# A transformer layer's last normalization: one column block of the last row tile, and one step of the other tile, over GpSimd and ScalarE

## The chip, the core and the metric

The kernel runs on one core of a Trainium2 chip. A core has a matrix engine (TensorE, PE in the profile, with its weight loads as PEld), a vector engine (VectorE, DVE), a scalar engine (ScalarE, ACT), a general engine (GpSimd, POOL) and SyncE (SP), which here only issues transfers. The engines run side by side, each through its own list of instructions in order, and wait for each other by semaphores. The metric is the device time of one execution in microseconds; lower is better.

## The reference

One encoder layer on 256 rows of width 2048: attention, a normalization, an MLP of width 8192, a second normalization. What matters here is the last line, the second normalization:

```python
def layer_norm(x, g, b):
    xf = x.astype(jnp.float32)
    mu = jnp.mean(xf, axis=-1, keepdims=True)
    var = jnp.mean(jnp.square(xf - mu), axis=-1, keepdims=True)
    y = (xf - mu) * lax.rsqrt(var + LN_EPS)
    return (y * g.astype(jnp.float32) + b.astype(jnp.float32)).astype(x.dtype)
...
        y = sq_relu_mlp(hff, mlp_w1[i], mlp_b1[i], mlp_w2[i], mlp_b2[i])
        x = layer_norm(DEEPNORM_ALPHA * x + (1.0 + g_f[:, None, :]) * y, ln_mlp_g[i], ln_mlp_b[i])
```

## The kernel before

The 256 rows are two row tiles of 128 rows (t = 0 and 1), one row on each partition. The 2048 columns are four column blocks of 512 (c = 0 to 3). `part(xs, t, c)` is one such piece, 128x512 in float32. `xs` has one buffer for each c, with both row tiles in it: in the listings of instructions g_2615 is c = 0, g_2617 is c = 1, g_2619 is c = 2 and g_2621 is c = 3. Most of the kernel is a stream of weights from HBM, split into a high and a low part by ScalarE and VectorE, with three matmuls of TensorE for each product (`mm3`, lines 556 to 558). This case is about its last 15 us.

There the last products of the MLP come out for c = 3, first for row tile 0, then for row tile 1. Those of row tile 1 are finished in two halves of 256 columns, so that the sums of the first half can be taken while TensorE works on the second. `add_gated` (lines 836 to 844) multiplies a product by the gate into `tmp` (line 841), adds it to the row (842) and takes its statistics (844). Then the row tile is closed:

- Row tile 0: `deviation` (lines 860 to 875) makes the mean and variance `mv` from the statistics (864), the root `sd` on ScalarE (866), and a refined reciprocal root `qq` by three small VectorE steps (871, 873, 874). Line 1358 makes (z - mean) * g for each block, line 1359 multiplies by `rstd` and adds b, and `store` (1342 to 1344) writes the block out. These are scalar_tensor_tensor instructions on VectorE: two tensors and one number for each row.
- Row tile 1: three blocks (c = 0, 1, 2) go over TensorE. `scaled` (1346) has put -z * g / 2 in place earlier, line 1384 copies it into PSUM by a product with the identity, and line 1397 adds mean * g / 2 by a product with `dm`, a diagonal matrix of the means (line 1391). Line 1398 then multiplies by `rstd` and adds b. The fourth block, c = 3, comes too late for this. For it line 1392 makes (z - mean) * `gneg` on VectorE while ScalarE takes the root, where `gneg` is -g / 2 (line 1364), and line 1398 multiplies and adds as for the others. The order of the blocks is 3, 1, 2, 0.

What sets the order: the framework's scheduler orders each engine's list by its own estimates of cost. `high_priority(200)` puts the statistics of row tile 1 ahead of older work, and `keep_in_program_order` (`keep`, `kept`) fixes the order of the closing steps on their engines. Nothing fixes the order of the stores. Odd c are issued from SP, even c from ScalarE (line 1343), and each queue issues them in the order of its list: a store that waits holds back those behind it. The program ends when the last store has landed.

Of the kernel before, what the change touches and what calls it, by code (L numbers as in the profile page):

```python
# [14 lines left out]
AF = mybir.ActivationFunctionType  # L15
OP = mybir.AluOpType
# [45 lines left out]
def hybrid_kernel(ctx: ExitStack, tc: tile.TileContext, a, out: bass.AP):  # L62
    nc = tc.nc
# [23 lines left out]
    def g4(dt=F32):  # L87
        return gen.tile([128, 1024], dt, tag="g4", name="g4")
# [102 lines left out]
    def first(name):  # L191
        n = AHEAD.get((stage[0], name), AHEAD.get(name))
        return tc.high_priority(n) if n else nullcontext()
# [356 lines left out]
    acc, xts, held, xs = {}, {}, {}, [None] * 4  # L550

    def part(tiles, t, c):
        return tiles[c][:, t * 512:t * 512 + 512]
# [303 lines left out]
    def kept(i):  # L857
        return tc.keep_in_program_order(i) if tight[0] else i

    def deviation(st=None, mv=None, between=lambda: None):  # L860
        with first("deviation"):
            if mv is None:
                mv = sml.tile([128, 2], F32, name="mv")
                kept(nc.vector.bn_aggr(mv, st))
            sd = sml.tile([128, 1], F32, name="sd")
            kept(nc.scalar.activation(sd, mv[:, 1:2], AF.Sqrt, bias=eps))
            ve = sml.tile([128, 1], F32, name="ve")
            kept(nc.vector.tensor_scalar_add(ve, mv[:, 1:2], LN_EPS))
            between()
            r0 = sml.tile([128, 1], F32, name="r0")  # L870
            kept(nc.vector.reciprocal(r0, sd))
            q = sml.tile([128, 1], F32, name="qq")
            kept(nc.vector.scalar_tensor_tensor(q, r0, ve, r0, op0=OP.mult, op1=OP.mult))
            kept(nc.vector.scalar_tensor_tensor(q, q, -3.0, r0, op0=OP.add, op1=OP.mult))
        return mv, q
# [463 lines left out]
    def affine(c):  # L1339
        return (gb[n][c // 2][:, (c % 2) * 512:(c % 2) * 512 + 512] for n in range(2))  # L1340

    def store(t, c, z):
        q = nc.sync if c % 2 else nc.scalar
        q.dma_start(out[t * 128:t * 128 + 128, c * 512:c * 512 + 512], z)
# [9 lines left out]
    mv, rstd = deviation(st[0][:, :4])  # L1354
    nc.vector.tensor_scalar_mul(rstd, rstd, -0.5)
    for c in (1, 0, 2, 3):
        z, (g, b) = part(xs, 0, c), affine(c)
        nc.vector.scalar_tensor_tensor(z, z, mv[:, 0:1], g, op0=OP.subtract, op1=OP.mult)
        nc.vector.scalar_tensor_tensor(z, z, rstd, b, op0=OP.mult, op1=OP.add)
        store(0, c, z)  # L1360
    for c in range(3):
        scaled(1, c)
    gneg = sml.tile([128, 512], F32, name="w", tag="t2", bufs=4)
# [17 lines left out]
    pw = {}  # L1381
# [4 lines left out]
    keep = tc.keep_in_program_order  # L1386
    with tc.high_priority(200):
        mv = sml.tile([128, 2], F32, name="mv")
        keep(nc.vector.bn_aggr(mv, st[1][:, :5]))
        dm = sml.tile([128, 128], F32, name="dm", tag="t2", bufs=4)  # L1390
        keep(nc.vector.tensor_scalar(dm, ident, mv[:, 0:1], 0.5, op0=OP.mult, op1=OP.mult))
        rstd = deviation(mv=mv, between=lambda: keep(nc.vector.scalar_tensor_tensor(
            part(xs, 1, 3), part(xs, 1, 3), mv[:, 0:1], gneg, op0=OP.subtract, op1=OP.mult)))[1]
    for c in (3, 1, 2, 0):
        z, (g, b) = part(xs, 1, c), affine(c)
        if c < 3:
            nc.tensor.matmul(pw[c], dm, g, start=False, stop=True)
        keep(nc.vector.scalar_tensor_tensor(z, pw.get(c, z), rstd, b, op0=OP.mult, op1=OP.add))
        store(1, c, z)


# [91 lines left out]
```

## Time and profile before

| | us |
|---|---|
| median of three runs (1067.41 to 1068.13) | 1067.83 |
| the profiled execution, its own time | 1066.71 |
| its span, first to last instruction | 1064.9 |
| last VectorE instruction ends | 1061.29 |
| granted TensorE clock over the span | 0.999 |

| engine | busy us | share of the span |
|---|---|---|
| TensorE matmuls | 1051.9 | 99% |
| VectorE | 941.2 | 88% |
| ScalarE | 619.9 | 58% |
| GpSimd | 27.5 | 3% |

A chain of waits is read backwards: from the last instruction to what released it, and so on. Its rows give a start, a duration on the chain, an engine, the tile written and the line. A timeline shows instructions in order of time; equal ones that follow each other are one row with a count, and their starts may overlap the end of the one before. A row of groups gives busy time and the mean of one instruction in ns. SPq and ACTq are the issue of transfers by SP and ScalarE; the transfer itself comes after. The profiled execution's own time stands 1.81 us above its span.

### The profile page before, as it was taken

The numbers are of one execution on the slowest core, as the hardware profiler recorded it, in microseconds if no ns is written. First come the engines' busy times: TensorE is split into PE (matmuls) and PEld (weight loads), VectorE is DVE, ScalarE is ACT, GpSimd is POOL, SyncE is SP. The second block draws the span as 40 slices with busy tenths as digits, with TensorE's granted clock in tenths as the row PEclk, the third lists the DMA queues.
The fourth block names the chain that finished last, engine by engine and source line by source line (L and its number), as shares of the span: only waits on it lengthen the run. The fifth ranks groups of instructions, "written<-read, shape, count | busy, mean of one in ns | idle before, by whom it ended". The sixth has DMA issues, their size and how long they took to land.

```text
span 1064.9 us, 16015 instructions
## 1 busy us (share of the span) xinstructions
PE 1051.9 (99%) x6181; PEld 856.6 (80%) x6181; DVE 941.2 (88%) x1407; ACT 619.9 (58%) x976; POOL 27.5 (3%) x54
## 2 busy tenths in 40 slices
PE   9999999999999999999999999999999999999998
PEld 7677677666677899988888888888888888888886
DVE  4689899989999998988579999889898987999998
ACT  5433347776772647643367776447677546777740
POOL 1000000001000000000000000000000001000000
PEclk9999999999999999999999999999999999999999
DMA  9999997799965897799625644974564783465742
GB/s 383 426 424 425 425 426 300 288 375 357 391 250 198 341 380 301 275 325 344 246 90 188 237 176 179 358 275 156 200 230 158 296 319 132 170 237 198 250 185 79
DMA packets 43516, 292.72 MB, mean 275 GB/s; under 512 B 5152, under 2 KB 5280, under 8 KB 9648
## 3 DMA queue, kind: packets, MB, share of 16 engines
q1 hardware_dynamic: 39456, 279.85, 67.6%
q0 software_dynamic: 3232, 10.50, 2.9%
q10 hardware_dynamic: 752, 1.35, 0.4%
q8 instruction: 48, 0.79, 0.3%
q14 instruction: 28, 0.23, 0.1%
HBM read 289.57 MB, written 2.11 MB: 274 GB/s over the span
## 4 chain that ended last, share of the span: by engine, by line
PE 92%; DVE 4%; ACT 2%; DMA 1%; issue 0%; DVEq 0%; ACTq 0%
PE pa L1189 17%; PE pa L556 16%; PE pa L558 15%; PE pa L557 15%; PE pa L1191 9%; PE pm L363 3%; PE pa L1163 3%; PE pa L1162 3%; PE pa L1161 3%; PE pa L769 2%; PE pa L830 1%; PE pt L813 1%; PE pa L666 1%; PE pt L557 1%; PE pt L556 1%; PE pt L558 1%
## 5 line engine op out<-in xcount | busy, mean ns | idle before, releaser
L299 ACT CAST wh<-raw 128x1024 fp32r<-128x1024 f32 (+1 forms) x332 | 336.2, 1020 | 264.5 <-PE pa L558 136.6
L250 DVE TENSOR_TENSOR wl<-raw,wh 128x1024 fp32r<-128x1024 f32 (+1 forms) x332 | 388.8, 1182 | 70.0 <-ACT wh L299 63.8
L556 PE MATMUL pa<-wh,g 128*128 128x512 f32 (+1 forms) x652 | 259.0, 398 | 4.8 <-ACT g L579 4.8
L557 PE MATMUL pa<-wl,g 128*128 128x512 f32 (+1 forms) x652 | 254.0, 390 | 0.0
L558 PE MATMUL pa<-wh,g 128*128 128x512 f32 (+1 forms) x652 | 253.2, 390 | 0.2 <-DVE g L581 0.2
L1189 PE MATMUL pa<-g,wh 128*128 128x512 f32 x768 | 191.3, 391 | 0.0
L1189 PEld LDWEIGHTS pa<-g,wh 128*128 128x128 f32 x768 | 140.7, 188 | 27.9 <-issue 0.8
L556 PEld LDWEIGHTS pa<-wh,g 128*128 128x128 f32 x652 | 122.4, 188 | 42.2 <-ACT g L579 6.4
L558 PEld LDWEIGHTS pa<-wh,g 128*128 128x128 f32 x652 | 122.4, 188 | 28.2 <-issue 1.6
L557 PEld LDWEIGHTS pa<-wl,g 128*128 128x128 f32 x652 | 122.6, 188 | 24.4 <-DVE scm L444 0.4
L1191 PEld LDWEIGHTS pa<-g,wl 128*128 128x128 f32 x768 | 104.8, 190 | 7.5
L1191 PE MATMUL pa<-g,wl 128*128 128x256 f32 x768 | 107.1, 282 | 0.0
L403 DVE SCALAR_TENSOR_TENSOR g<-raw,cact,g 128x1024 f32<-128x1024 f32 (+1 forms) x69 | 86.2, 1257 | 0.7 <-DMA raw<-in_modm 0.3
L1161 PE MATMUL pa<-g,wh 128*128 128x256 f32 x240 | 67.7, 284 | 0.2 <-ACT wh L299 0.2
L1163 PE MATMUL pa<-g,wh 128*128 128x256 f32 x240 | 67.6, 285 | 0.0
L1162 PE MATMUL pa<-g,wl 128*128 128x256 f32 x240 | 67.4, 284 | 0.0
L250 DVE TENSOR_TENSOR raw<-raw 128x1024 fp32r<-128x1024 f32 x48 | 58.4, 1222 | 0.7 <-ACT raw L299 0.6
L299 ACT CAST raw<-raw 128x1024 fp32r<-128x1024 f32 x48 | 49.9, 1045 | 5.6 <-DVE raw L261 4.3
L403 DVE SCALAR_TENSOR_TENSOR g4b<-raw,cact,g4b 128x1024 f32<-128x1024 f32 x32 | 40.6, 1280 | 6.9 <-DMA raw<-in_modgf 6.9
L1162 PEld LDWEIGHTS pa<-g,wl 128*128 128x128 f32 x240 | 45.8, 192 | 0.6 <-issue 0.4
L1161 PEld LDWEIGHTS pa<-g,wh 128*128 128x128 f32 x240 | 45.8, 192 | 0.4 <-ACT wh L299 0.4
L1163 PEld LDWEIGHTS pa<-g,wh 128*128 128x128 f32 x240 | 45.8, 192 | 0.1
(235 smaller groups left out, 1273.5 us busy)
## 6 DMA issues: line engine op xcount, KB each, us to landing
raw<-in_w1b SPq DMA_DIRECT2D x48, 1024.0 KB, 6.6
raw<-in_w SPq DMA_DIRECT2D x40, 1024.0 KB, 7.6
raw<-in_modm SPq DMA_DIRECT2D x32, 1024.0 KB, 12.6
raw<-in_modf SPq DMA_DIRECT2D x32, 1024.0 KB, 7.0
raw<-in_wqkv SPq DMA_DIRECT2D x24, 1024.0 KB, 14.3
raw<-in_w2s SPq DMA_DIRECT2D x24, 1024.0 KB, 4.9
raw<-in_modgm SPq DMA_DIRECT2D x16, 1024.0 KB, 7.1
raw<-in_wo SPq DMA_DIRECT2D x16, 1024.0 KB, 7.4
```

Source lines behind the costliest of these rows:

```text
L250: self.pinned(nc.vector.tensor_sub(l[:, :w], r, f32(self.hs[n])[:, :w]))
L299: self.pinned(nc.scalar.copy(h[:, :s.shape[-1]], s))
L363: i = nc.tensor.matmul(self.ps[32 * j:32 * j + 32, :w], lhsT[j] if type(lhsT) is list else lhsT, rhs[j], start=self.first, stop=stop)
L403: nc.vector.scalar_tensor_tensor(p[:, :e], s, cact[:, kt:kt + 1], p[:, :e], op0=OP.mult, op1=OP.add)
L556: nc.tensor.matmul(ps, xh, wh, start=start, stop=False)
L557: nc.tensor.matmul(ps, xh, wl, start=False, stop=False)
L558: S.prev = nc.tensor.matmul(ps, xl, wh, start=False, stop=stop).ins
L1161: nc.tensor.matmul(o, wh(w, 128), hh, start=new, stop=False)
L1162: nc.tensor.matmul(o, wl(w, 128), hh, start=False, stop=False)
L1163: nc.tensor.matmul(o, wh(w, 128), hl, start=False, stop=end)
L1189: nc.tensor.matmul(ps, wh(k, 128), ff_in(k), start=k == 0, stop=False)
L1191: nc.tensor.matmul(ps[:, :256], wl(k, 128), ff_in(k)[:, :256], start=False, stop=k == NK - 1)
```

## The change

Row tile 0, block c = 3: the last step (multiply by `rstd`, add b) is split. ScalarE multiplies by `rstd` in place, GpSimd adds b.

Row tile 1, block c = 3: none of it is left to VectorE. GpSimd makes z * gneg into a new buffer `side` (its first half, `zg`), ScalarE makes gneg * mean into the other half (`mg`), GpSimd subtracts, ScalarE multiplies by `rstd`, GpSimd adds b into z. The order of the blocks in the source is now 1, 3, 2, 0.

```diff
     for c in (1, 0, 2, 3):
         z, (g, b) = part(xs, 0, c), affine(c)
         nc.vector.scalar_tensor_tensor(z, z, mv[:, 0:1], g, op0=OP.subtract, op1=OP.mult)
-        nc.vector.scalar_tensor_tensor(z, z, rstd, b, op0=OP.mult, op1=OP.add)
+        if c < 3:
+            nc.vector.scalar_tensor_tensor(z, z, rstd, b, op0=OP.mult, op1=OP.add)
+        else:
+            nc.scalar.activation(z, z, AF.Copy, scale=rstd)
+            nc.gpsimd.tensor_tensor(z, z, b, op=OP.add)
         store(0, c, z)
...
-        rstd = deviation(mv=mv, between=lambda: keep(nc.vector.scalar_tensor_tensor(
-            part(xs, 1, 3), part(xs, 1, 3), mv[:, 0:1], gneg, op0=OP.subtract, op1=OP.mult)))[1]
-    for c in (3, 1, 2, 0):
+        side = g4()
+        zg, mg = side[:, :512], side[:, 512:]
+        nc.gpsimd.tensor_tensor(zg, part(xs, 1, 3), gneg, op=OP.mult)
+        rstd = deviation(mv=mv)[1]
+        keep(nc.scalar.activation(mg, gneg, AF.Copy, scale=mv[:, 0:1]))
+        nc.gpsimd.tensor_tensor(zg, zg, mg, op=OP.subtract)
+    for c in (1, 3, 2, 0):
         z, (g, b) = part(xs, 1, c), affine(c)
         if c < 3:
             nc.tensor.matmul(pw[c], dm, g, start=False, stop=True)
-        keep(nc.vector.scalar_tensor_tensor(z, pw.get(c, z), rstd, b, op0=OP.mult, op1=OP.add))
+            keep(nc.vector.scalar_tensor_tensor(z, pw[c], rstd, b, op0=OP.mult, op1=OP.add))
+        else:
+            keep(nc.scalar.activation(zg, zg, AF.Copy, scale=rstd))
+            nc.gpsimd.tensor_tensor(z, zg, b, op=OP.add)
         store(1, c, z)
```

Lines below 1359 move down by up to 11: 1384 becomes 1388, 1391 becomes 1395, 1397 becomes 1405, and 1398 becomes 1406.

GpSimd's and ScalarE's lists at the end of the program, after the change. g_10059 is `side`, w is `gneg`, g_9694 holds b of blocks 2 and 3; the names in brackets are the semaphores waited for.

```order
L1363 TENSOR_TENSOR g_2621<-g_2621,g_9694 128x512 [waits DMASW1_49,Activation_49]
L1398 TENSOR_TENSOR g_10059<-g_2621,w 128x512 [waits DVE_49,PE_49]
L1401 TENSOR_TENSOR g_10059<-g_10059 128x512 [waits Activation_49,Pool_49]
L1409 TENSOR_TENSOR g_2621<-g_10059,g_9694 128x512 [waits Activation_49]
```

```order
L866 ACTIVATE sd<-mv,eps 128x1 [waits DVE_49]
L1362 ACTIVATE g_2621<-g_2621,qq 128x512 [waits DVE_49]
L1344 DMA out<-g_2615 128x512 [waits DVE_49]
L1344 DMA out<-g_2619 128x512 [waits DVE_49]
L866 ACTIVATE sd<-mv,eps 128x1 [waits DVE_49]
L1400 ACTIVATE g_10059<-w,mv 128x512 [waits PE_49]
L1408 ACTIVATE g_10059<-g_10059,qq 128x512 [waits DVE_49,Pool_49]
L1344 DMA out<-g_2619 128x512 [waits DVE_49]
L1344 DMA out<-g_2615 128x512 [waits DVE_49]
```

GpSimd had no instruction here before, ScalarE only the two roots (866) and the four stores; no load of a function table is added on ScalarE.

VectorE's list at the same place, with what is taken out (-) and the rows around it:

```order
 L844 BN_STATS st_9700<-g_2621 128x6 [waits DVE_49]
-L1359 SCALAR_TENSOR_TENSOR g_2621<-g_2621,qq,g_9694 128x512
 L841 TENSOR_TENSOR tmp<-pa,g4b 128x256 [waits PE_49]
...
-L1392 SCALAR_TENSOR_TENSOR g_2621<-g_2621,mv,w 128x512
...
-L1398 SCALAR_TENSOR_TENSOR g_2621<-g_2621,qq,g_9694 128x512 [waits DVE_49]
```

Three scalar_tensor_tensor instructions leave VectorE; the order of the rest is as before.

SP's list of stores, before and then after the change. The first two rows of each are row tile 0, the last two row tile 1.

```order
L1344 DMA out<-g_2617 128x512 [waits DMASW1_49,DVE_49]
L1344 DMA out<-g_2621 128x512 [waits DMAHW0_49,DMASW3_49,DVE_49]
L1344 DMA out<-g_2621 128x512 [waits DMAHW1_49,DVE_49]
L1344 DMA out<-g_2617 128x512 [waits DMAHW2_49,DVE_49]
```

```order
L1344 DMA out<-g_2617 128x512 [waits DMASW1_49,DVE_49]
L1344 DMA out<-g_2621 128x512 [waits DMASW3_49,Pool_49]
L1344 DMA out<-g_2621 128x512 [waits DMAHW1_49,Pool_49]
L1344 DMA out<-g_2617 128x512 [waits DMAHW2_49,DVE_49]
```

The order is the same, block 3 before block 1, though the source of the changed kernel has block 1 first. What is new is that block 3's store waits for GpSimd, with block 1's store behind it.

## The prediction, made before the changed kernel was run

> **What bounds the kernel now.** First the page: how long the span is and what the chain that ended last is made of.
>
> ```profile
> span 1064.9 us, 16015 instructions
> PE 92%; DVE 4%; ACT 2%; DMA 1%; issue 0%; DVEq 0%; ACTq 0%
> ```
>
> Matmuls carry 92% of the chain, and the change touches none of them. What it can move lies behind the last product, so I read the chain of waits from 1051 us on (start, duration on the chain, engine, tile, line).
>
> ```profile
> 1050.98 2.08 DVE g L1359 x3
> 1053.06 0.67 DVE tmp L841 x2
> 1053.73 0.67 DVE g L842 x2
> 1054.39 0.34 DVE st L844
> 1054.73 0.65 DVE g L1359
> 1055.38 0.34 DVE tmp L841
> 1055.75 0.43 DVE g L842
> 1056.21 0.44 DVE st L844
> 1056.67 0.30 DVE mv L1389
> 1057.00 0.29 DVE dm L1391
> 1057.34 0.66 DVE g L1392
> 1058.00 0.08 DVE r L871
> 1058.11 0.23 DVE qq L873
> 1058.37 0.17 DVE qq L874
> 1058.56 2.07 DVE g L1398 x3
> 1060.63 0.66 DVEq L1489
> ```
>
> VectorE alone, without a gap; the last row is its fourth L1398, which ends at 1061.29. Behind it come stores. The timeline of the two issuing queues and the stretches of the close (the last two numbers are the busy share of the DMA engines and GB/s):
>
> ```profile
> 1059.34 0.99 SPq L1344 DMA_DIRECT2D out<-g  x2
> 1060.66 1.00 ACTq L1344 DMA_DIRECT2D out<-g  x2
> 1059.20:1060.00 0.80, 0.80 (x3) 0.15 (x1) 0.80 (x3) 0.00 (x0) 0.00 (x0) 1.00 0.00 0
> 1060.00:1062.00 2.00, 0.18 (x1) 0.00 (x0) 1.29 (x2) 0.00 (x0) 0.00 (x0) 1.00 0.93 350
> 1062.00:1063.10 1.10, 0.00 (x0) 0.00 (x0) 0.00 (x0) 0.00 (x0) 0.00 (x0) 1.00 0.91 313
> 1063.10:1064.90 1.80, 0.00 (x0) 0.00 (x0) 0.00 (x0) 0.00 (x0) 0.00 (x0) 0.69 0.01 2
> ```
>
> The first of the last four stores is issued at 1059.34 and nothing moves before 1060.00: 0.66 us from issue to data. Then the DMA engines are over 90% busy until about 1063.05: four blocks of 0.26 MB (0.70 + 0.34 MB by the rates) in 3.05 us, 0.76 each. So the end isn't simply VectorE's end plus a transfer. The four stores are one packed block of 3.05 us that begins 0.66 us after the **first** of them is issued. A last store issued a little earlier gains nothing; a first store issued later costs its whole delay. From the last data to the span's end it is 1064.9 - 1063.05 = 1.85 us, which I carry over.
>
> **What the change takes off VectorE.** Row tile 0: the L1359 at 1054.73 (0.65 us). Row tile 1: L1392 (0.66) and one L1398 (0.66). Together 1.97 us of a gapless chain, but other work stands right behind:
>
> ```profile
> 1054.61 0.28 PE L558 MATMUL pa<-g4b,g 128*128 128x256 f32 x1
> 1054.72 2.74 PE L1384 MATMUL pa<-g,ident 128*128 128x512 f32 x6
> 1057.34 2.84 PE L1397 MATMUL pa<-g,dm 128*128 128x512 f32 x6
> ```
>
> The last product ends at 1054.89, so the second-half L841 can't start before 1054.92; at best it comes 0.40 earlier in effect (alone it needs 0.41 instead of the chain's 0.34). The identity products step at 0.43 each (2.74 less 0.59 for the last, over five), so the first `dm` product can start at 1057.30 at the earliest; the third block's product then ends near 1060.07, against 1060.18 now. TensorE becomes the next limit.
>
> **What it adds.** The price of ScalarE's step stands in the trace, that of GpSimd's doesn't:
>
> ```profile
> L801 ACT ACTIVATE g<-g,rs 128x256 f32<-128x256 f32 x64 | 28.0, 508 | 3.2 <-DVE rs L795 3.0
> L866 ACT ACTIVATE sd<-mv,eps 128x1 f32<-128x1 f32 x4 | 1.2, 295 | 37.8 <-DVE mv L864 27.4 <-DVE mv L1389 8.9 <-DVE r L871 1.5
> L171 POOL TENSOR_SCALAR_AFFINE_SELECT g<-g 128x768 f32<-128x768 f32 x2 | 1.8, 876 | 0.0
> L124 POOL TENSOR_SCALAR_AFFINE_SELECT sc<-sc 128x128 f32<-128x128 f32 x1 | 0.3, 300 | 0.0
> L123 POOL MEMSET sc<- 128x512 f32 x1 | 0.5, 537 | 0.0
> ```
>
> L801 is the same function with a number for each row; 256 columns more at about 0.84 ns (508 less 295, over 255) make 0.72 us for 512. GpSimd's select reads one tensor: 0.90 ns a column ((876 - 300) / 640) and 0.18 fixed, so 0.65 us for 512. That is the lower bound P of a two-input step (second input free). Twice the whole is 1.29, twice the column part only 1.11; with a write on top that costs as much as a memset it is 1.29 + 0.53 = 1.82, the upper bound. I take **P = 1.2**, between 1.11 and 1.29, since both inputs have to be read. [...] A wait that ends on GpSimd costs 0.07:
>
> ```profile
> 299.09 0.69 DVE L952 SCALAR_TENSOR_TENSOR g<-g,g4b 128x512 f32<-128x512 f32 x1
> 299.85 0.95 POOL L384 MEMSET g4b<- 128x1024 f32 x1 [37.50 <-DVE g L952]
> ```
>
> **Do GpSimd and VectorE run side by side?** GpSimd is idle in this stretch before, and nowhere in the trace does it read a tensor beside a VectorE step with two SBUF inputs. So both ends are open: no cost, or they take turns for whole instructions. [...]
>
> ```profile
> L842 DVE TENSOR_TENSOR g<-g,tmp 128x512 f32<-128x512 f32 x1 | 0.7, 684 | 0.0
> L1364 DVE TENSOR_SCALAR w<-g 128x512 f32<-128x512 f32 x1 | 0.4, 418 | 0.0
> ```
>
> [...]
>
> **The sum, step by step (P = 1.2, turns).**
> 1. Row tile 0. ScalarE multiplies 1050.98 to 1051.70. GpSimd's add (L1363) is ready at 1051.77, while VectorE runs three L1360 that follow each other without a gap (three of 0.75 in 2.08 us, so each starts before the last has ended). I let it wait for their end: 1053.13 to 1054.33. L841 doesn't care, but L842 waits to 1054.33 instead of 1053.73, +0.60. L1359 is gone, -0.65. The second-half L841 starts at 1055.34: 0.04 gained, where 0.40 was to be had.
> 2. Row tile 1. L842 ends at 1056.14, GpSimd's z * gneg runs 1056.21 to 1057.41. The mean is there at 1056.93; `dm`, ready to go, waits to 1057.41 and ends at 1057.70, 0.41 later than before. TensorE's products shift with it: 1058.88, 1059.74, 1060.60.
> 3. ScalarE: root to 1057.25, gneg * mean (0.72) to 1057.99. VectorE: L868, L871, then L873 to 1058.10. GpSimd's subtraction, ready at 1058.06, gets its turn then, 1058.10 to 1059.30; L874 waits behind it to 1059.47, 0.93 later than the 1058.54 of before, although L1392's 0.66 is gone.
> 4. VectorE: three L1406 of 0.66 to 0.75, blocks 1, 2, 0 done at 1060.20, 1060.87, 1061.54 (before: 1061.29). ScalarE's multiplication 1059.49 to 1060.21, GpSimd's add 1060.28 to 1061.48.
> 5. Stores. Block 3 from SP at 1061.51. Block 1 is done at 1060.20, but stands behind block 3 in SP's list, so goes at 1061.86. Block 2 from ScalarE at 1060.90 is now the first, block 0 at 1061.58. The packed block starts 1060.90 - 1059.34 = **1.56 us** later, and all four keep it fed.
>
> The span becomes 1066.4, the profiled execution 1066.71 + 1.5 = 1068.2. The median before lies 1.1 above its profiled run, so I forecast a median of 1067.83 + 1.5 = **1069.3**. That is 0.14%; under 0.2% (2.1 us) a measurement of this kernel can't tell it from no change.
>
> **The rivals.**
> - *GpSimd's step is dearer.* Steps 1 to 4 hold P four times, nearly three of them on the path. At 1.82, L842 is freed at 1054.95, z * gneg ends at 1058.65, the subtraction at 1060.80, L874 at 1061.25; block 2's store goes at 1062.68: +3.35, 1071.2. It passes +2.1 at about P = 1.40; with P near 1.6 it is 1070.5. For it: no row of such a step, and three of them in series with ScalarE. Against: 1.82 needs reads and writes to add up. **This is the slower side, 0.33.**
> - *GpSimd goes ahead of the third L1360.* It has waited since 1051.77 and might take the gap at 1052.39. Then the third L1360 runs after it, the second half starts at 1056.0 instead of 1055.34, and all of the rest shifts: +2.2, 1070.0. Against: the overlapped starts. 0.13, half of it over 2.1.
> - *Side by side.* No turns: L841 at 1054.92, `qq` at 1057.47, products at 1058.35, 1059.20, 1060.07, VectorE done at 1060.84. GpSimd's chain: 1055.85 to 1057.05, gneg * mean to 1057.64, subtraction to 1058.91, ScalarE to 1059.65, add to 1060.92. Block 2's store is first at 1060.00 and the next comes at 1060.87, so data end near 1063.8: +0.8, 1068.6. 0.15.
> - *Not slower.* Side by side with P = 0.65 block 3 goes at 1059.85. If in addition the four transfers don't queue for the DMA engines, the end follows the last store, block 0 at 1060.87 against 1061.32: -0.45, 1067.4. Against: over 90% busy in the rows above. 0.04, of which 0.01 could exceed 0.2%.
>
> **How the numbers follow.** Forecast 0.35, dearer 0.33, ahead 0.13, side by side 0.15, not slower 0.04. Slower by over 0.2%: 0.33 + 0.07 = 0.40. Within: 0.35 + 0.06 + 0.15 + 0.03 = 0.59. Faster: 0.01. The range reaches from below side by side with a cheaper step (1067.9) to the upper bound of P (1071.3).
>
> **What would show it.** Step 1: L842 of the first half starting only as L1363 ends, with VectorE idle between. Step 2: `dm` starting as L1398 on GpSimd ends. Step 3: L874 or L873 standing until L1401 ends. If VectorE runs through all three without a gap, turns are wrong. Step 5: first data near 1061.6, and SP's last two stores 0.35 us apart just after GpSimd's last add. The forecast is wrong if GpSimd's step is outside 1.0 to 1.4 us, or if block 3's store leaves before block 2's.

## The result and the profile after

| | before | after |
|---|---|---|
| median of 22 runs each, us | 1067.64 (1066.72 to 1069.61) | 1069.57 (1068.27 to 1071.77) |
| span of the profiled execution, us | 1064.9 | 1067.7 |
| row tile 0's L1355 ends, us | 1050.96 | 1051.87 |
| the close: from there to the span's end, us | 13.94 | 15.83 |

The ratio of times is 1.0016, with a 95% interval of 1.0011 to 1.0022: slower by 1.7 us (1.2 to 2.4). The two profiled spans differ by 2.8 us, but 0.91 of that lies ahead of the changed code, before L1355 ends, where both kernels do the same work. So I measure every kernel here by its **close**: from the end of row tile 0's L1355 in the chain of waits to the end of the span. By it the change costs 1.89 us. A close comes from one execution and the spans are given to a tenth, so differences under 0.1 say little, even where figures agree to the hundredth. Times given below as "after L1355" count from its end in the timeline, 0.01 earlier (1050.95 and 1051.86).

The page of the changed kernel, its span and the engines of the chain that ended last:

```profile
span 1067.7 us, 16024 instructions
PE 90%; DVE 4%; ACT 2%; DMA 2%; issue 1%; DVEq 0%; ACTq 0%
```

Matmuls still carry the chain. The chain of waits of the changed kernel behind row tile 0's L1355 (start, duration on the chain, engine, tile, line):

```profile
1051.89 3.12 DVE g L1360 x3
1055.01 0.67 DVE tmp L841 x2
...
1057.96 0.30 DVE mv L1393
...
1058.28 0.67 DVE dm L1395
1058.95 0.06 DVE ve L868
...
1059.12 0.23 DVE qq L873
...
1059.37 1.25 DVE qq L874
...
1060.71 1.41 DVE g L1406 x2
```

The chain is still VectorE's alone, without a gap over 0.04, and it never names GpSimd. By the prediction's own sign (VectorE running through without a gap) turns would be wrong. But three of its rows have grown: three steps on row tile 0 from 2.08 to 3.12, `dm` from 0.29 to 0.67, and L874, a step on 128x1, from 0.17 to 1.25. Here VectorE's wait for GpSimd, which is not for a semaphore, leaves no idle time; it is inside the duration of the waiting instruction. I say that an instruction stands while it is recorded as running but waits in this way. What VectorE stands for is seen when GpSimd's rows of the timeline are laid beside it (start, duration, line, tiles, shape, idle time before and what ended it):

```profile
1052.70 1.76 POOL L1363 TENSOR_TENSOR g<-g,g 128x512 f32<-128x512 f32 x1 [50.33 <-ACT g L1362]
1057.60 1.26 POOL L1398 TENSOR_TENSOR g<-g,w 128x512 f32<-128x512 f32 x1 [3.14 <-PE pa L1388]
1059.33 1.26 POOL L1401 TENSOR_TENSOR g<-g 128x512 f32<-128x512 f32 x1 [0.47 <-ACT g L1400]
1061.50 1.27 POOL L1409 TENSOR_TENSOR g<-g,g 128x512 f32<-128x512 f32 x1 [0.91 <-ACT g L1408]
```

A GpSimd step takes 1.26 us. L1398 ends at 1058.86 and `dm` at 1058.95; L1401 ends at 1060.59 and L874 at 1060.61. For L1363, the view of L1360 alone (duration in ns, min/median/max):

```profile
L1360 DVE SCALAR_TENSOR_TENSOR g<-g,qq,g x3: 747/754/1783, 1051.9 to 1053.2; 128x512 f32<-128x512 f32 x3
```

Two of the three take what they took before, the third 1.04 more. L1363 is recorded from 1052.70, but its 1.76 is 0.50 above the other steps: it stood until about 1053.20, when the second L1360 (1052.56 to 1053.31 by its record) was all but over, and then went ahead of the third. The third is recorded from 1053.22 and ends at 1055.01, 0.55 behind L1363's end. L1406, which reads one tensor from PSUM, is not longer beside L1409 (2.07 for three, 2.06 before):

```profile
1060.71 2.07 DVE L1406 SCALAR_TENSOR_TENSOR g<-pa,qq,g 128x512 f32<-128x512 f32 x3
```

ScalarE's work, and the issue of the last four stores (ACTq, then SPq):

```profile
1051.89 0.72 ACT L1362 ACTIVATE g<-g,qq 128x512 f32<-128x512 f32 x1 [2.86 <-DVE qq L1355]
1060.70 0.72 ACT L1408 ACTIVATE g<-g,qq 128x512 f32<-128x512 f32 x1 [1.51 <-DVE qq L874]
1062.15 1.01 ACTq L1344 DMA_DIRECT2D out<-g  x2
1062.80 0.83 SPq L1344 DMA_DIRECT2D out<-g  x2
```

The stretches of the end, first one of the kernel before, then those of the changed kernel (the last two numbers are the DMA engines' share and GB/s):

```profile
1060.00:1060.66 0.66, 0.18 (x1) 0.00 (x0) 0.66 (x2) 0.00 (x0) 0.00 (x0) 1.00 0.74 289
1062.80:1063.00 0.20, 0.00 (x0) 0.00 (x0) 0.00 (x0) 0.00 (x0) 0.00 (x0) 1.00 0.00 0
1063.00:1064.00 1.00, 0.00 (x0) 0.00 (x0) 0.00 (x0) 0.00 (x0) 0.00 (x0) 1.00 1.04 399
1064.00:1065.00 1.00, 0.00 (x0) 0.00 (x0) 0.00 (x0) 0.00 (x0) 0.00 (x0) 1.00 1.04 387
1065.00:1065.50 0.50, 0.00 (x0) 0.00 (x0) 0.00 (x0) 0.00 (x0) 0.00 (x0) 0.79 1.07 381
1065.50:1066.00 0.50, 0.00 (x0) 0.00 (x0) 0.00 (x0) 0.00 (x0) 0.00 (x0) 0.50 0.39 143
```

The first store (block 2) is issued at 1062.15 and its data move from 1063.0, 0.85 later; by the share of the last row the last data land near 1065.7. In the kernel before, a share of 0.74 in the 0.66 us from 1060.00 puts the first data near 1060.17, 0.83 after the issue at 1059.34. The prediction read 0.66 there, from the edge of its stretch; the true figure is nearly the same in both kernels, so this does not touch the difference.

**Where the 1.97 us went that VectorE was rid of.** Given back as stands: 1.04 (third L1360) + 0.38 (`dm`) + 1.08 (L874) = 2.50. VectorE's last step ends 10.92 after L1355, against 10.34 before, +0.58; 2.50 less 1.97 is 0.53 of it. The other 1.3 of the +1.89 come behind VectorE: block 1 is finished first, near 1061.46, but its store waits on SP behind block 3's until about 1063.2, so the first of the four stores is block 2's and leaves 10.29 after L1355, against 8.39. Of these 1.90, 1.24 are there because the first closing step on VectorE starts later (L1406 at 8.85 after L1355, against 7.61 for L1398), and 0.66 because block 2's store goes first in place of block 1's.

### The profile page after: what moved, and what is told of

Same layout as the page of the kernel before. It is cut to its first block, busy times and chain, and to the rows that moved or that the text cites. A ratio compares the mean times of both kernels' runs of the same rounds, so it can differ in the third digit from the quotient of the medians.

```text
span 1067.7 us, 16024 instructions
## 1 busy us (share of the span) xinstructions
PE 1054.8 (99%) x6181; PEld 858.3 (80%) x6181; DVE 941.9 (88%) x1404; ACT 621.5 (58%) x979; POOL 33.1 (3%) x58
## 4 chain that ended last, share of the span: by engine, by line
PE 90%; DVE 4%; ACT 2%; DMA 2%; issue 1%; DVEq 0%; ACTq 0%
PE pa L556 16%; PE pa L1189 15%; PE pa L558 15%; PE pa L557 15%; PE pa L1191 8%; PE pm L363 4%; PE pa L1163 3%; PE pa L1162 3%; PE pa L1161 3%; PE pa L769 2%; PE pa L830 1%; PE pt L813 1%; PE pa L666 1%; ACT wh L299 1%; PE pt L557 1%; PE pt L556 1%
## 5 line engine op out<-in xcount | busy, mean ns | idle before, releaser
L250 DVE TENSOR_TENSOR wl<-raw,wh 128x1024 fp32r<-128x1024 f32 (+1 forms) x332 | 388.8, 1182 | 68.3 <-ACT wh L299 62.5
L1189 PEld LDWEIGHTS pa<-g,wh 128*128 128x128 f32 x768 | 140.5, 188 | 28.3 <-issue 0.8
L250 DVE TENSOR_TENSOR raw<-raw 128x1024 fp32r<-128x1024 f32 x48 | 58.4, 1222 | 0.7 <-ACT raw L299 0.6
L1161 PEld LDWEIGHTS pa<-g,wh 128*128 128x128 f32 x240 | 45.9, 192 | 0.4 <-ACT wh L299 0.4
L599 DVE TENSOR_TENSOR g<-g,pa 128x512 f32<-128x512 f32 x60 | 39.6, 682 | 7.4 <-PE pa L558 7.0
```

The source lines that it names most:

```text
L250: self.pinned(nc.vector.tensor_sub(l[:, :w], r, f32(self.hs[n])[:, :w]))
L1161: nc.tensor.matmul(o, wh(w, 128), hh, start=new, stop=False)
L1189: nc.tensor.matmul(ps, wh(k, 128), ff_in(k), start=k == 0, stop=False)
```

## The experiments

The theory: GpSimd and VectorE take turns for whole instructions wherever VectorE's step reads two tensors from SBUF, or one at the doubled rate; three such collisions, and the order of the stores, make up the 1.89 us. The doubled rate is that of L1364, which takes 418 ns for one tensor of 512 columns, where L842 takes 684 for two. By the column it is 0.53 ns in the kernel before (L401, one tensor: 479 ns for 512 columns, 749 for 1024), against 1.03 (L250, two tensors: 691 and 1220). The main rivals: GpSimd's steps are simply too long in series, or the first of the four stores alone sets the end.

| kernel | what differs | median us (before beside it) | ratio, 95% interval | close us |
|---|---|---|---|---|
| after | the change | 1069.57 (1067.64) | 1.0016 [1.0011, 1.0022] | 15.83 |
| e1 | row tile 0's part alone | 1067.64 (1067.47) | 0.9997 [0.9989, 1.0006] | 14.38 |
| e2 | row tile 1's part alone | 1068.57 (1067.47) | 1.0012 [1.0003, 1.0022] | 15.42 |
| e3 | after, `qq` in steps with one SBUF tensor | 1068.75 (1067.47) | 1.0011 [1.0003, 1.0020] | 15.6 |
| e4 | after, block 1's store ahead of block 3's | 1068.06 (1067.47) | 1.0003 [0.9995, 1.0012] | 15.04 |
| e5 | e3, `dm` in 127 and 1 columns | 1069.22 (1067.32) | 1.0016 [1.0007, 1.0025] | 15.63 |
| e6 | row tile 1's part with e3 to e5 | 1068.65 (1067.32) | 1.0007 [0.9998, 1.0016] | 14.65 |
| e7 | after, row tile 0's add held back | 1068.49 (1067.32) | 1.0014 [1.0004, 1.0023] | 15.3 |
| e8 | before, block 3's step and store in halves | 1067.59 (1067.32) | 1.0001 [0.9992, 1.0010] | 13.9 |
| e9 | before, row tile 0's add on GpSimd in two held halves | 1067.01 (1067.19) | 0.9996 [0.9988, 1.0005] | 13.65 |
| e10 | after, `dm` from an identity in PSUM | 1068.76 (1067.19) | 1.0014 [1.0005, 1.0023] | 15.48 |
| e11 | before, `dm` in 127 and 1 columns | 1066.90, one run | none | 14.05 |

Most ratios differ by less than their intervals. What tells the experiments apart is the trace.

### e1 and e2: the two parts alone

e1 has the first hunk of the diff and not the others, e2 the others and not the first. In e2 the two stores on SP are held in the order that they have in the changed kernel:

```diff
-        store(1, c, z)
+        if c == 3:
+            keep(store(1, 3, z))
+            keep(store(1, 1, part(xs, 1, 1)))
+        elif c != 1:
+            store(1, c, z)
```

> Row tile 0's part of the change alone; row tile 1 as before. The close is counted from the end of L1355 to the end of the span: 13.94 us before, 15.83 in the changed kernel. Theory (GpSimd and VectorE take turns for whole instructions): the third multiply-add of row tile 0 stands behind GpSimd's add and takes some 1.78 us instead of 0.75 (+1.04), the fourth one's 0.65 is gone, so everything behind comes 0.39 later: close 14.33, time +0.4 us against the kernel before. Rival (the loss sits in row tile 1 alone, and the long third step is an accident of one execution): close 13.5 to 13.6, since L1359's 0.65 is taken away and up to 0.40 of it counts; time -0.4.

> Row tile 1's part alone, with SP's stores held in the changed kernel's order (block 3, then block 1); row tile 0 as before. Theory (turns): the three steps of row tile 0 take 0.75 each, dm takes 0.67 instead of 0.29, L874 1.24 instead of 0.16; close 13.94 + 1.89 - 0.39 = 15.44, time +1.5 us against before. Rival (the two parts aren't additive; row tile 1's loss comes from GpSimd being late by row tile 0's add): close under 14.5, time within 0.5 us of before.

VectorE's timeline of e1, row tile 0:

```profile
1050.85 3.12 DVE L1360 SCALAR_TENSOR_TENSOR g<-g,qq,g 128x512 f32<-128x512 f32 x3
```

and of e2:

```profile
1050.90 2.08 DVE L1359 SCALAR_TENSOR_TENSOR g<-g,qq,g 128x512 f32<-128x512 f32 x3
1056.92 0.70 DVE L1391 TENSOR_SCALAR dm<-ident,mv 128x128 f32<-128x128 f32 x1
1058.04 1.21 DVE L874 SCALAR_TENSOR_TENSOR qq<-qq,r 128x1 f32<-128x1 f32 x1
```

The long third step goes with row tile 0's part, the long `dm` and L874 with row tile 1's. The costs add: 14.38 and 15.42 are 0.44 and 1.48 above 13.94, together 1.92, and the whole change has 1.89. So the loss has two independent parts, and most of it is row tile 1's.

### e3: steps for `qq` with one SBUF tensor

If two SBUF tensors are what makes L873 and L874 wait, the same arithmetic with numbers for each row must not wait:

```diff
+            if tight[0]:
+                kept(nc.vector.tensor_scalar(q, r0, ve, r0, op0=OP.mult, op1=OP.mult))
+                kept(nc.vector.tensor_scalar(q, q, -3.0, r0, op0=OP.add, op1=OP.mult))
```

> The changed kernel, but the two small steps L873 and L874 of row tile 1 are written with one tensor and numbers for each row instead of two tensors (same arithmetic). Theory (turns count for VectorE steps that read two SBUF tensors): the second small step takes 0.15 to 0.25 us instead of 1.24 while GpSimd's subtraction still runs beside it; TensorE's products then set the last three steps, block 2's store goes 0.4 us earlier, close 15.4. Rival (any VectorE step from SBUF stands while GpSimd reads): still about 1.2 us, close 15.8.

The timeline of e3, GpSimd, VectorE, ScalarE (L875 is the step that was L874):

```profile
1058.67 1.26 POOL L1405 TENSOR_TENSOR g<-g 128x512 f32<-128x512 f32 x1 [0.46 <-ACT g L1404]
1058.76 0.21 DVE L875 TENSOR_SCALAR qq<-qq,r 128x1 f32<-128x1 f32 x1
1059.50 2.47 DVE L1410 SCALAR_TENSOR_TENSOR g<-pa,qq,g 128x512 f32<-128x512 f32 x3 [0.53 <-PE pa L1409]
1059.96 0.72 ACT L1412 ACTIVATE g<-g,qq 128x512 f32<-128x512 f32 x1 [1.44 <-POOL g L1405]
```

L875 runs inside GpSimd's step, in 0.21 instead of 1.24: the second SBUF tensor was the cause. The close falls by only 0.23, though. VectorE now waits for TensorE's product (0.53 idle), and ScalarE waits for GpSimd's subtraction instead of for `qq`. Counted from the start of the close, L875 ends 0.97 sooner than L874 in the changed kernel (7.78 and 8.75), and the first L1410 starts 0.54 sooner than the first L1406 (8.31 and 8.85): taking the stand away uncovers the next wait.

### e4: the order of the stores

```diff
-        store(1, c, z)
+        if c % 2:
+            keep(store(1, c, z))
+        else:
+            store(1, c, z)
```

> The changed kernel with SP's last two stores in the order block 1, block 3. Theory of the packed block (the first of the four stores sets the end): block 1's store goes as its step ends, 0.7 us before block 2's, the transfers start 0.7 us earlier; since block 3's store still goes last at the same time, the end comes 0.4 to 0.75 us earlier: close 15.1 to 15.4. Rival (the end follows the last store and GpSimd's last add): the last store goes 0.35 us earlier at most, close 15.5 to 15.8.

Issue on the two queues of e4, and the end of its data:

```profile
1061.29 1.64 SPq L1344 DMA_DIRECT2D out<-g  x2
1061.95 1.02 ACTq L1344 DMA_DIRECT2D out<-g  x2
1062.00:1062.50 0.50, 0.00 (x0) 0.00 (x0) 0.50 (x1) 0.00 (x0) 0.50 (x1) 1.00 0.74 291
1064.50:1065.00 0.50, 0.00 (x0) 0.00 (x0) 0.00 (x0) 0.00 (x0) 0.00 (x0) 1.00 0.71 246
```

No instruction got shorter; block 1's store leaves as soon as it is ready, 0.66 ahead of block 2's. The close falls by 0.79, to 15.04, a little more than the 0.4 to 0.75 expected. Of the single repairs to the changed kernel this is worth the most.

### e5 and e11: `dm` in 127 and 1 columns

e5 is e3 with `dm` split so that the long piece has an odd number of columns, meant to take it off the doubled rate; that an odd number would do so was the author's estimate. If the rate is what makes `dm` stand, the long piece then runs beside GpSimd's step:

```diff
+        for s in (slice(0, 127), slice(127, 128)):
+            keep(nc.vector.tensor_scalar(dm[:, s], ident[:, s], mv[:, 0:1], 0.5, op0=OP.mult, op1=OP.mult))
```

> As the run with one-input small steps, and dm is written in two pieces of 127 columns and 1 column, so that it can't go two columns at a time (same values). [...] Rival (any VectorE step that reads SBUF with a number for each row stands there): the first piece still ends with GpSimd's multiplication, some 0.65 us.

The timeline of e5:

```profile
1057.29 0.79 DVE L1400 TENSOR_SCALAR dm<-ident,mv 128x127 f32<-128x127 f32 x2
1056.61 1.27 POOL L1403 TENSOR_TENSOR g<-g,w 128x512 f32<-128x512 f32 x1 [3.15 <-PE pa L1392]
```

The two pieces still took 0.79, the long one 0.67 of it, until GpSimd's step was over at 1057.88. That could mean that the theory is wrong, or that 127 columns still go at the doubled rate. e11 puts the same split into the kernel before, where GpSimd is idle.

> The kernel before with dm in pieces of 127 columns and 1 column: it tells how long these pieces take with GpSimd idle. If 127 columns go one at a time the first piece takes 0.35 us, and its 0.67 beside GpSimd speaks against the doubled rate as the reason; if it takes 0.29, the odd piece still went at the doubled rate, and that run told nothing about it.

The view of e11's `dm` (duration in ns, min/median/max):

```profile
L1392 DVE TENSOR_SCALAR dm<-ident,mv x2: 207/246/286, 1057.1 to 1057.3; 128x127 f32<-128x127 f32 x1, 128x1 f32<-128x1 f32 x1
```

127 columns take 0.286, all 128 take 0.29 in the kernel before, and the 1 column takes 0.207, so 0.63 ns for each column more: the rate had not changed, and e5 says nothing about the theory. Its long `dm` is what turns would give.

### e10: `dm` from PSUM

The same question with another lever: the identity is read from PSUM, put there by one product ahead of time.

```diff
+    ip = psm.tile([128, 512], F32, name="pm")
+    tc.keep_in_program_order(nc.tensor.matmul(ip[:, :128], ident, ident, start=True, stop=True))
...
-        keep(nc.vector.tensor_scalar(dm, ident, mv[:, 0:1], 0.5, op0=OP.mult, op1=OP.mult))
+        keep(nc.vector.tensor_scalar(dm, ip[:, :128], mv[:, 0:1], 0.5, op0=OP.mult, op1=OP.mult))
```

> The changed kernel, but dm is made from a copy of the identity in PSUM (one more small product on TensorE, some 0.2 us, ahead of the identity products). [...] Rival (any VectorE step stands while GpSimd multiplies, or dm waits for something else): it still ends just after GpSimd's multiplication, 0.67 us.

GpSimd and VectorE in e10:

```profile
1058.66 1.27 POOL L1400 TENSOR_TENSOR g<-g,w 128x512 f32<-128x512 f32 x1 [3.15 <-DVE g L842]
1059.41 0.35 DVE L1397 TENSOR_SCALAR dm<-pm,mv 128x128 f32<-128x128 f32 x1
1060.18 0.16 DVE L874 SCALAR_TENSOR_TENSOR qq<-qq,r 128x1 f32<-128x1 f32 x1
1060.38 1.27 POOL L1403 TENSOR_TENSOR g<-g 128x512 f32<-128x512 f32 x1 [0.46 <-ACT g L1402]
1060.98 2.47 DVE L1408 SCALAR_TENSOR_TENSOR g<-pa,qq,g 128x512 f32<-128x512 f32 x3 [0.64 <-PE pa L1407]
```

`dm` starts and ends inside GpSimd's step. At 0.35 it is slower than the 0.29 from SBUF and faster than the 0.67 of standing. It also brings L874 ahead of the subtraction, which starts at 1060.38, so both stands are gone at once. Yet the close falls by only 0.35: as in e3, VectorE then waits for TensorE.

### e6: all repairs together

Row tile 0 as before, row tile 1 moved, with e3's steps, e5's split and e4's order of stores.

> Row tile 1's part of the change, with row tile 0 as before, one-input small steps, dm in two odd pieces, and SP's stores in the order block 1, block 3: every wait found so far taken away, but GpSimd and ScalarE still make block 3. Theory: the parts add up, 15.42 (row tile 1 alone) - 0.79 (order of stores) - 0.23 to 0.5 (small steps, dm) = 14.1 to 14.4, time +0.2 to +0.5 us against before, no gain, since block 3 still needs three GpSimd steps of 1.26 in series. Rival (without the waits the 1.3 us taken from VectorE count): close 13.3 to 13.6, time -0.4 to -0.6.

VectorE's `dm` and GpSimd's last step for block 3 in e6:

```profile
1057.69 0.82 DVE L1396 TENSOR_SCALAR dm<-ident,mv 128x127 f32<-128x127 f32 x2
1060.83 1.26 POOL L1410 TENSOR_TENSOR g<-g,g 128x512 f32<-128x512 f32 x1 [0.83 <-ACT g L1409]
```

The close is 14.65, above what was expected and still 0.71 over the kernel before. `dm` stood all the same (0.82 for its two pieces). And block 3 remains three GpSimd steps of 1.26 and two ScalarE steps of 0.72, 5.05 us from the first start (1057.04) to the last end (1062.09), in place of two VectorE steps of 0.66. So the small steps and the order of the stores are worth 0.77 of row tile 1's 1.48; no run separates what `dm` and block 3's long way have in the other 0.71. If the parts add up, an estimate for e10's `dm` together with row tile 0 as before and e4's order is 15.48 - 0.44 - 0.79 = 14.25, which would leave some 0.3 for the long way. The rival that GpSimd's steps are too long in series is therefore not out, but it is the smaller part.

### e7 and e9: row tile 0's add at a better place

In e7 the add is held until the second L842 of the first half has ended:

```diff
-            nc.gpsimd.tensor_tensor(z, z, b, op=OP.add)
+            late = z, b
...
+                i = nc.gpsimd.tensor_tensor(late[0], *late, op=OP.add)
+                tc.add_manual_dep(i.ins, done.ins.name, AFTER, reason="not sooner")
```

> The changed kernel, with GpSimd's add of row tile 0 held until the second L842 of the first half has ended; the steps behind it are one that takes statistics (one input) and L841 (one input from PSUM). Theory (turns): the third multiply-add is back at 0.75 us, the statistics and L841 run beside GpSimd undisturbed (0.42 and 0.41), and the next L842 stands until GpSimd's 1.26 us are over, so its end comes where it was before the change: close 15.83 - 0.39 = 15.4. Rival (VectorE slows down whenever GpSimd reads): the statistics or L841 take longer than 0.5, close 15.7 or more.

GpSimd and VectorE in e7:

```profile
1054.57 1.27 POOL L1387 TENSOR_TENSOR g<-g,g 128x512 f32<-128x512 f32 x1 [53.08 <-DVE g L842]
1051.02 2.08 DVE L1361 SCALAR_TENSOR_TENSOR g<-g,qq,g 128x512 f32<-128x512 f32 x3
1054.97 0.42 DVE L841 TENSOR_TENSOR tmp<-pa,g4b 128x256 f32<-128x256 f32 x1 [0.20 <-PE pa L558]
1055.42 0.70 DVE L842 TENSOR_TENSOR g<-g,tmp 128x256 f32<-128x256 f32 x1
```

The third step has its 2.08 back. L841, with one tensor in PSUM, runs beside GpSimd in its usual 0.42; L842, with two in SBUF, stands to 1056.12 where GpSimd ends at 1055.84. The step is too long for the gap by 0.28. So e9 cuts it in two, each half held until an L842 ended, in the kernel before and with nothing else of the change:

```diff
+            s = slice(h * 256, h * 256 + 256)
+            i = nc.gpsimd.tensor_tensor(late[0][:, s], late[0][:, s], late[1][:, s], op=OP.add)
+            tc.add_manual_dep(i.ins, done.ins.name, AFTER, reason="not sooner")
```

> The kernel before, with only row tile 0's last step of block 3 moved: ScalarE multiplies, GpSimd adds b in two halves of 256 columns, each held until a VectorE L842 has ended, so that it runs beside steps that take statistics or read PSUM. Theory (turns, only for VectorE steps with two SBUF inputs or at the doubled rate): no VectorE step gets longer, L1359's 0.65 is gone, the second-half L841 waits for the last product and starts 0.40 earlier in effect; the last three steps then stand on TensorE; close 13.5 to 13.65 against 13.94, time -0.3 to -0.4 us, too little for the runs to tell, so the trace decides. Rival (GpSimd work in the close always costs VectorE what it saves): close 13.9 or more.

GpSimd in e9, and VectorE beside it:

```profile
1054.32 0.73 POOL L1387 TENSOR_TENSOR g<-g,g 128x256 f32<-128x256 f32 x1 [53.07 <-DVE g L842]
1055.68 0.72 POOL L1387 TENSOR_TENSOR g<-g,g 128x256 f32<-128x256 f32 x1 [0.64 <-DVE g L842]
1055.18 0.42 DVE L842 TENSOR_TENSOR g<-g,tmp 128x256 f32<-128x256 f32 x1
1056.42 0.29 DVE L1401 TENSOR_SCALAR dm<-ident,mv 128x128 f32<-128x128 f32 x1
```

Both halves lie between VectorE's steps of two SBUF tensors, and none of those is longer. VectorE does not wait for TensorE in its last steps either, although the expectation had it so. The close is 13.65, 0.29 under the kernel before: the only version that gains in the trace. In time it is 0.9996 [0.9988, 1.0005], which the runs can't tell from no change.

### e8: the first store earlier

The prediction has the first store set the end. In the kernel before, block 3's step and store are cut in two, so that the first leaves earlier:

```diff
+            for h in range(2):
+                s = slice(h * 256, h * 256 + 256)
+                keep(nc.vector.scalar_tensor_tensor(z[:, s], z[:, s], rstd, b[:, s], op0=OP.mult, op1=OP.add))
+                nc.sync.dma_start(out[128:256, 1536 + h * 256:1792 + h * 256], z[:, s])
```

> The kernel before, with block 3's last step of row tile 1 and its store in two halves of 256 columns. Theory of the packed block: the first transfer starts 0.3 to 0.4 us earlier, VectorE ends 0.08 later, and since the DMA engines are full from there on, the end comes 0.2 to 0.35 us earlier: close 13.6 to 13.75 against 13.94. Rival (the end follows the last store): close 14.0, 0.08 later.

The stretches of e8 (start of data, the gap, the end):

```profile
1061.00:1061.50 0.50, 0.50 (x2) 0.00 (x0) 0.50 (x2) 0.00 (x0) 0.00 (x0) 1.00 0.24 88
1061.50:1062.00 0.50, 0.13 (x1) 0.00 (x0) 0.50 (x2) 0.00 (x0) 0.00 (x0) 1.00 0.77 268
1062.00:1062.50 0.50, 0.00 (x0) 0.00 (x0) 0.50 (x2) 0.00 (x0) 0.00 (x0) 1.00 0.64 230
1064.00:1064.50 0.50, 0.00 (x0) 0.00 (x0) 0.00 (x0) 0.00 (x0) 0.00 (x0) 1.00 0.95 352
```

The first store leaves 8.13 after L1355 instead of 8.39 and data move earlier, but with gaps, and the last land near 1064.48, which is 12.09 after L1355, against 12.10 in the kernel before (1063.05). The close of 13.9 misses the theory's 13.6 to 13.75 and can't be told from the rival's 14.0: a first store that leaves earlier gains nothing here. An account that fits both this and e4: a transfer of 0.26 MB starts 0.83 after its issue or when the one ahead of it ends, whichever is later, and takes about 0.69 (at the 381 to 399 GB/s of the changed kernel). In the kernel before, stores come every 0.66 and hardly queue, so first and last set the end together, although the engines are busy without a gap (shares of 0.93 to 1.06 from 1060.50 to 1063.00); in the changed kernel four come within 1.1 us and queue behind the first. The account gives the end of the data to within about 0.1 in the kernel before, the changed one, e4 and e8; it is an account, not something a run took apart.

## Why the prediction came out as it did

The median was forecast at 1069.3 as 1.5 over the kernel before; it came 1069.57, and the ratio puts the difference at 1.7 (1.2 to 2.4). That less than 0.2% can't be told from no change was wrong for 22 runs each: the interval, 1.0011 to 1.0022, excludes no change. Point by point:

- **GpSimd's step, P = 1.2** (bounds 0.65 and 1.82): 1.26. "Dearer P" would have needed 1.40 to pass 2.1 us. The halves of e9 show how it is made up: 0.725 for 256 columns and 1.26 for 512 leave 0.19 fixed beside 2.1 ns a column.
- **Turns, for whole instructions:** right. Which steps take them was the author's estimate, which no row of the kernel before shows; what lies behind them no run shows. The runs show which steps they are, e3, e7 and e10 from both sides: steps with one SBUF tensor or one in PSUM (L875 in e3, 0.21; L844 and L841 in e7, 0.42 each; `dm` from PSUM, 0.35; the last L1406, 2.07 for three) run beside GpSimd's step, those with two (third L1360, 1.78; L842 in e7, 0.70; L874) stand until it ends, down to a 128x1 step that took 1.24 us instead of 0.16 (L874). For `dm` on the doubled rate, e10 moved its input and the stand went. That changed the place and the rate together (0.35 for 0.29); that the rate is what counts rests on L875 and L844, which read one tensor from SBUF and ran free. L844 goes at 1.02 ns a column in the kernel before (424 ns for 256, 685 for 512), and in e9 it took its usual 0.43 (from 1055.64) beside GpSimd's second half (1055.68 to 1056.40). The signs named for it were the wrong ones: there is no idle time, `dm` does not start as L1398 ends, and VectorE runs through without a gap, because the stand is inside the durations. Side by side, which put the time at 1068.6, is out.
- **Step 1 failed in its order.** "I let it wait for their end" was wrong: GpSimd went in between the second L1360 and the third, the order of the rival "ahead of the third L1360". The second half's L841 starts 4.74 after L1355 instead of 4.35, +0.39, where I had -0.04. The overlapped starts, my argument against, give VectorE no precedence: L1363 is recorded from 1052.70 and the third L1360 from 1053.22, so GpSimd had come first, and step 1 did not apply to it the rule by which it made `dm` and L874 wait. The rival's size was too big (+0.70 there, +2.2 at the end): L1363 got its turn at 1053.20, and the third step needed only 0.55 behind it.
- **Step 2,** `dm` ends 0.41 later: 0.75 (7.09 after L1355, against 6.34). The step alone became 0.38 longer; the rest is step 1's 0.39.
- **Step 3,** L874 ends 0.93 later: 1.17. Here the 0.43 missed in step 1 came in, but 0.18 of it went again between the mean and `qq`: 2.36 us from the end of the aggregate to the end of L874 (1058.25 to 1060.61), where I had 2.54. I let L874 run its whole 0.17 after GpSimd's end; it took 0.02, and the subtraction started 0.09 sooner after the mean, against 0.06 for the longer P.
- **Step 4:** order of the blocks and ScalarE's 0.72 as forecast; L1406 and L1409 side by side, as forecast.
- **Step 5,** block 2's store first and 1.56 later: it was first, and 1.90 later. Of the 0.34 more, 0.24 is L874 and the rest the start of L1406. SP's last two stores came just behind GpSimd's last add, 0.42 apart instead of 0.35. "A first store issued later costs its whole delay" held: 1.90, and the close grew by 1.89; e4 gave 0.79 back. That the first store sets the end held only where the stores queue; in the kernel before it did not, as e8 shows, though its DMA engines are busy without a gap too.

So turns, their places in row tile 1 and the order of the stores were right; the order in row tile 0 was the rival's, and the sum was 0.3 to 0.4 low in the trace: 0.43 from that order, partly made good in step 3. That the median came within 0.3 of the forecast is in part luck: the close grew by 1.89, between the forecast's 1.5 and that rival's 2.2, and a little nearer the rival's. The profiled span was forecast at 1066.4 and came out at 1067.7; 0.91 of those 1.3 us lie ahead of the changed code and have nothing to do with it. As to who goes first: in every collision here it was the step whose record starts first. L1363 went ahead of the third L1360 in all six kernels that have the add there (the changed one, e1, e3, e4, e5, e10), L1401 (1059.33) ahead of L874 (1059.37), and the add of e7 (1054.57) ahead of L842 (1055.42); the other way round, L1363 itself stood 0.50 while the second L1360, recorded from 1052.56, was running. In none of these do the two start together.

## What to carry to other kernels

Before moving an elementwise step from VectorE to GpSimd, list the VectorE steps that will run beside it, and mark those with two SBUF tensors or on the doubled rate: here each that met a GpSimd step under way stood until that was over (L874, on 128x1, for 1.08 of its 1.26), and the cost hid inside its duration in the profile. Among such steps a GpSimd step left VectorE alone here only in a gap as long as itself, so cut it to the gap and hold it there (e9, 0.29 us in the trace and too little for the runs to tell), or give the neighbours one tensor in PSUM or a number for each row (e10, `dm` 0.35 for 0.67; e3, L875 0.21 for 1.24). When a chain's order is changed, look at the order of the stores on each queue: here one store behind a later block cost 0.8 of the 1.9 us.

## What the runs showed of the hardware that was not expected

- A GpSimd step that waited for VectorE (L1363, in six kernels) went in between two VectorE steps whose recorded durations overlap (0.75 each, 0.66 apart). Both the waiting and the overtaken instruction are recorded as running: 1.76 for a step of 1.26, 1.78 for one of 0.75. What a standing VectorE step still needed behind GpSimd's end went by its columns: 0.55 us for 512 (third L1360), 0.28 for 256 (L842 in e7), 0.02 for 1 (L874).
- An odd number of columns kept the doubled rate: 0.286 us for 127 in e11, 0.287 for 128 in the kernel before.
- A block's store cut into two halves did not use the DMA engines as well: 268 and 230 GB/s in e8, where whole blocks went at 387 and 375 in the kernel before (1060.66 to 1062.00). Part of this are gaps between issues; the runs don't separate that from the shorter rows.
